# Nine of eleven swiglu blocks by seven products instead of eight, with six fill-in units in most turns and A12 ahead of F3

## The chip, the cores and the metric

One core of one Trainium2 chip. The metric is the device time of one execution in microseconds; lower is better. Times are the median of three runs. The profile is of one execution, with a span from the first to the last instruction.

## The reference

Two layers on an input of 256 tokens by 2048, fp32. Each layer adds a token mixer (a gated linear attention in layer 0, a sparse attention in layer 1) and then a swiglu, both on the RMS-normed input. Weights are read once from HBM. The change touches only the swiglu, with D_FF = 5632:

```
def swiglu(h, w1, w3, w2):
    return (jax.nn.silu(h @ w1) * (h @ w3)) @ w2

for i in range(DEPTH):                      # DEPTH = 2
    ...
    x = x + swiglu(rmsnorm(x, norm_ffn[i]), ffn_w1[i], ffn_w3[i], ffn_w2[i])
```

## The kernel before

All large products run in three fp32r matmuls: each operand is split into a high part and the rest, and hi*hi, hi*lo and lo*hi are added in PSUM. For weights this is `split_w`: a 1 MB tile (128 x 4 x 512) is cast on ACT to `wh` (line 137), then VectorE subtracts to get `wl` (line 138). `wh` and `wl` have three buffers each. Tiles that are used once come through the tag `raw`, which has four buffers (`RAW = 4`); the SP queue loads them. A unit of work that has 24 matmuls of 128x512 is called a step below.

The swiglu works on 11 blocks of 512 columns of w1 and w3. The tokens are two tiles of 128 and the inner dimension is cut in two halves, so that the pair (h @ w1 block, h @ w3 block) is a product of 2x2 block matrices:

- The plain way (`plain_steps`, matmuls at line 475, PSUM tile `half`) takes 8 block products, in 8 units of 24 matmuls each. Each unit splits one raw tile and uses it for both token tiles.
- The other way (`pair`, matmuls at line 398, PSUM tile `acc`) is a Strassen-Winograd form with 7 block products of 24 matmuls each, called A11, F5, F3, A12, F6, N7 and N22 after the combined activations that they use. Each product splits two weight tiles (chunk c = 0, 1), each for 12 matmuls. The combined weights are built on the way: `va` and `vb` are loaded to homes of their own (tags v0, v1, v2 and g3). During A11 VectorE adds `vb` to `va` (`plus`, line 411). During F5 and F6 POOL issues loads that add to `va` in flight (`plus_dma`, line 419). During F3 VectorE forms `-vb - vc` in `vb` (`minus`, line 415), `vc` being F3's own raw tiles; N7 reads the result. A12 has the raw tiles `vd`.

A sum on VectorE is not issued at once. `product` appends it to `sums_due`, and the next `split_w` issues it right behind its own subtraction:

```
        v = nc.vector.tensor_sub(wl, raw, wh.bitcast(F32))
        if sums_due:
            with behind((v.ins,)):
                sums_due.popleft()()
```

So the sum for F3's chunk 0 stands behind the split of F3's chunk 1, and that for chunk 1 behind the split of whatever comes next.

The down projection of finished blocks (`pieces`, matmuls at lines 531 to 533, PSUM tile `down`) is cut in units too, of one weight tile and 24 matmuls: four units a block. A piece of two blocks copies `x` into PSUM (line 521), runs two units, and copies back (line 538), four times; a piece of one block does so for every unit.

`ffn` runs the blocks with seven products one after the other, as turns. `pair` is a generator that yields after each product (slots 0 to 6) and once more (slot 7). After a slot, `ffn` calls `unit()` as many times as the slot stands in the turn's tuple, and each call takes the next unit from the list `todo`. Before, nearly every turn has a unit at each of the eight slots, two of them in a row at the end (slots 6 and 7). -1 in a tuple is a unit ahead of the turn. The gated results of a block are transposed in the following turn (`late`, `side`, `tick`, line 220) and kept in one of three tiles by `hi_lo(b % 3)`, until the down projection has read them. The last block's down projection is done after the turns.

The tile framework sets the order of the instructions in each engine's queue at build time from the program's order and from what is ready by its own estimate, and adds all semaphores. A tile is taken when its buffer is free.

Of the kernel before, what the change touches and what calls it, by code (L numbers as in the profile page):

```python
# [55 lines left out]
def trunk(  # L56
# [60 lines left out]
    def tick():  # L117

        while side:
            try:  # L120
                return next(side[0])
            except StopIteration:
                side.popleft()
# [9 lines left out]
    def split_w(raw, pool=wp):  # L133

        wh = pool.tile([P, 4, NB], F32R, tag="wh", bufs=3 if pool is wp else 1, name="wh")
        wl = pool.tile([P, 4, NB], F32R, tag="wl", bufs=3 if pool is wp else 1, name="wl")
        nc.scalar.copy(wh, raw)  # L137
# [4 lines that stand above are left out]
        return wh, wl  # L142
# [70 lines left out]
    def split_t(src, hi, lo):  # L213

        for kk in range(2):
            tr = tr_p.tile([P, 2, SEQ], F32, tag="tr", name="tr")
            for t in range(NT):
                for k in range(2):
                    c = (2 * kk + k) * P
                    nc.tensor.transpose(tr[:, k, t * P:(t + 1) * P], src[t][:, c:c + P], ident)  # L220
            sl = slice(2 * kk, 2 * kk + 2)
            nc.scalar.copy(hi[:, sl, :], tr)  # L222
            nc.vector.tensor_sub(lo[:, sl, :], tr, hi[:, sl, :].bitcast(F32))
            yield
# [139 lines left out]
    def hi_lo(i):  # L364
        g = res.tile([P, 2, 4, SEQ], F32R, tag=f"g{i}", name=f"g{i}")
        return g[:, 0], g[:, 1]
# [6 lines left out]
    def pair(nrm, wa, wb, c0, turn, done):  # L373

        def src(w, j, c):
            r = j * 1024 + c * 512
            return w[r:r + 512, c0:c0 + NB].rearrange("(k p) n -> p k n", p=P)

        def load(w, j, homes):
            o = []
            for c, (pool, tag, bufs) in enumerate(homes):
                raw = pool.tile([P, 4, NB], F32, tag=tag, bufs=bufs, name=tag)
                nc.sync.dma_start(raw, src(w, j, c))
                o.append(raw)
            return o

        def product(acc, raws, form, start, stop, then=None):
            for c in range(2):  # L390
                wh, wl = split_w(raws[c])
                if then is not None:
                    then(c)
                hi, lo = nrm.forms[form]
                for j in range(4):
                    k = 4 * c + j
                    for i, (l_, r_) in enumerate(((hi, wh), (hi, wl), (lo, wh))):
                        nc.tensor.matmul(acc, l_[:, k, :], r_[:, j, :], start=start and k == i == 0,  # L398
                                         stop=stop and k == 7 and i == 2, skip_group_check=not start)
                    if j % 2:  # L400
                        tick()

        def bank():
            return acc_p.tile([P, NB], F32, tag="acc", name="acc")

        def sums(tag):
            return nrm.pool.tile([P, NB], F32, tag=tag, bufs=1, name=tag)

        def plus(dst, other):

            return lambda c: sums_due.append(lambda: nc.vector.tensor_add(dst[c], dst[c], other[c]))  # L411

        def minus(dst, other):

            return lambda c: sums_due.append(lambda: nc.vector.scalar_tensor_tensor(
                dst[c], dst[c], -1.0, other[c], op0=ALU.mult, op1=ALU.subtract))

        def plus_dma(dst, w, j):
            return lambda c: nc.gpsimd.dma_start(dst[c], src(w, j, c), accum_op=ALU.add)

        fz = nrm.pool
        stream = [(wp, "raw", RAW)] * 2
        homes = [((fz, "v0", 1), (fz, "v1", 1)), ((fz, "v2", 1), (res, "g3", 1))]
        va = load(wa, 0, homes[turn])
        vb = load(wb, 0, homes[1 - turn])
        b1 = bank()
        product(b1, va, "A11", True, True, plus(va, vb))
        b3 = bank()
        nc.scalar.mul(b3, b1, -1.0)
        yield  # L430
        b2 = bank()
        product(b2, va, "F5", True, True, plus_dma(va, wb, 1))
        y = cm.tile([P, NB], F32, tag="u", name="u")
        nc.scalar.copy(y, b2)
        yield
        vc = load(wb, 1, stream)
        product(b2, vc, "F3", False, True, minus(vb, vc))
        yield
        vd = load(wa, 1, stream)
        product(b1, vd, "A12", False, True)  # L440
        done("11", b1)
        yield
        product(b3, va, "F6", False, True, plus_dma(va, wa, 1))
        w = sums("w")
        nc.scalar.copy(w, b3)
        nc.vector.tensor_add(w, w, b2)
        done("12", w)
        yield
        product(b3, vb, "N7", False, True)
        nc.vector.tensor_add(y, y, b3)  # L450
        yield
        product(b3, va, "N22", False, True)
        done("21", b3)
        done("22", y)
        yield
        yield
# [84 lines left out]
    def ffn(layer, nrm):  # L541

        w1, w3, w2 = ffn_w1[layer], ffn_w3[layer], ffn_w2[layer]
        sc = {}
        ready = set()
        late = []

        def block(b, us):
            def turned():
                yield from split_t(us, hi, lo)  # L550
                ready.add(b * NB)

            hi, lo = hi_lo(b % 3)
            late.append(turned())
            made[b] = hi, lo, b * NB

        def gate(us):
            def done(q, v):
                t = int(q[0]) - 1
                if q == "21":  # L560
                    nc.scalar.activation(v, v, AF.Silu, scale=sc["n"][:, 1:2])
                    us[t] = v
                elif q == "22":
                    nc.vector.scalar_tensor_tensor(v, v, sc["r"][:, 1:2], us[t], op0=ALU.mult, op1=ALU.mult)
                    us[t] = v
                elif q[1] == "1":
                    us[t] = cm.tile([P, NB], F32, tag="u", name="u")
                    nc.scalar.activation(us[t], v, AF.Silu, scale=sc["n" if t else "r"][:, t:t + 1])
                else:
                    nc.vector.scalar_tensor_tensor(us[t], us[t], sc["r"][:, t:t + 1], v, op0=ALU.mult, op1=ALU.mult)  # L570
            return done

        todo = deque()
        made = {}

        def unit():

            while True:
                kind, item, gen = todo[0]
                try:  # L580
                    got = next(gen)
                except StopIteration:
                    todo.popleft()
                    continue
                if got is not None:
                    made[item] = got[0]
                    late.append(got[1])
                return

        def filler(item):  # L590

            if isinstance(item, int):
                return "plain", item, plain_steps((w1, w3), item, nrm.forms, sc, ready)
            return "piece", item, pieces(w2, [made[b] for b in item], ready)

        full = (0, 1, 2, 3, 4, 5, 6, 7)
        turns = ((0, (-1, -1, 0, 1, 2, 4, 5, 6), (1,)), (2, full, ((1, 0),)), (3, full, (4,)), (5, full, ((2, 3),)),
                 (6, full, ((4, 5),)), (7, full, (8,)), (9, full, ((6, 7),)), (10, full, ((8, 9),)))
        for turn, (b, at, items) in enumerate(turns):
            todo.extend(filler(i) for i in items)  # L600
            us = [None] * NT
            for _ in range(at.count(-1)):
                unit()
            for slot, _ in enumerate(pair(nrm, w1, w3, b * NB, 1 - turn % 2, gate(us))):
                side.extend(late)
                late.clear()
                for _ in range(at.count(slot)):
                    unit()
                if turn == 0 and slot == 0:
                    flush()  # L610
                    sc["r"] = nrm.rstd()
                    sc["n"] = scaled(sc["r"], -1.0, "rq")
            block(b, us)
        for _, _, gen in todo:
            assert next(gen, None) is None
        side.extend(late)
        return w2, [made[10]]
# [557 lines left out]
```

## Time and profile before

| | |
|---|---|
| median of 3 runs | 2227.94 us (2227.71 to 2228.21) |
| the profiled execution's own time | 2227.94 us |
| its span | 2226.2 us |
| TensorE matmul busy | 2207.4 us |
| VectorE busy | 1545.1 us |
| ACT busy | 1289.2 us |
| data moved | 493.35 MB, mean 222 GB/s |

In the profile's rows PE is TensorE's matmuls, DVE is VectorE, ACT is ScalarE, and SPq and POOLq are the queues that issue loads. L398 is line 398 of the kernel. A timeline row has the start and the length in us, the engine, the line, the operation and its tiles, and in brackets the idle time before it and what ended it. A chain row has the start, the length and what was at work, with the number of instructions. Windows give the busy time of each engine in a stretch, the granted clock, the mean busy share of the 16 DMA engines, and GB/s. A row of waits has the total in us, the number of times and the longest. A matmul's own length in the trace is longer than its share of time, since matmuls overlap; the chain shows the share. A few matmul records can be missing.

### The profile page before, as it was taken

To read this page: it belongs to the slowest core of one execution; us is meant where nothing else is said; L and a number is where in the kernel's file an instruction comes from. 1 tells how busy PE (TensorE), PEld (TensorE's weight loads), DVE (VectorE), ACT (ScalarE), POOL (GpSimd) and SP (SyncE) were. 2 spreads that over 40 slices of the span, in tenths; PEclk is the share of its full clock that TensorE was granted. 3 is DMA by queue.
4 is the path that set the end of the run, shared out by engine and by line. 5 is a ranking of instruction groups with operands and counts; after the bars stand their busy time and mean duration, and the time that the engine had idled before them with its cause. 6 is when DMAs were issued, how large, how long until landed. Compare 5 with 4: busy or idle time off the path is not lost.

```text
span 2226.2 us, 25148 instructions
## 1 busy us (share of the span) xinstructions
PE 2207.4 (99%) x10199; PEld 1828.2 (82%) x10199; DVE 1545.1 (69%) x1180; ACT 1289.2 (58%) x1248; POOL 111.3 (5%) x157
## 2 busy tenths in 40 slices
PE   9999999999999999999999999999999999999998
PEld 7888888888888888888888888888888888888886
DVE  6546546887777777877655755557877777787776
ACT  5545445666656665666544445456666666666664
POOL 0000000000000000000100000000000000000000
PEclk9999999999999999999999999999999999999999
DMA  8555465889879879777554554466997897897893
GB/s 293 172 170 178 135 229 179 263 224 314 222 228 307 221 229 315 211 228 231 194 183 142 178 173 159 164 204 196 298 243 238 276 247 228 281 261 214 281 245 114
DMA packets 254773, 493.35 MB, mean 222 GB/s; under 512 B 8201, under 2 KB 20833, under 8 KB 254529
## 3 DMA queue, kind: packets, MB, share of 16 engines
q1 hardware_dynamic: 219856, 423.33, 54.4%
q0 software_dynamic: 33792, 67.11, 17.3%
q8 instruction: 80, 1.31, 0.2%
q10 hardware_dynamic: 1008, 1.31, 0.2%
q14 instruction: 37, 0.30, 0.0%
HBM read 489.59 MB, written 2.12 MB: 221 GB/s over the span
## 4 chain that ended last, share of the span: by engine, by line
PE 95%; DVE 2%; ACT 1%; issue 1%; DMA 0%; SPq 0%; POOL 0%; POOLq 0%; ACTq 0%
PE acc L398 26%; PE half L475 11%; PE acc L206 11%; PE acc L208 11%; PE acc L207 11%; PE down L533 7%; PE down L532 6%; PE down L531 6%; PE tr L220 1%; DVE wl L138 1%; ACT wh L137 1%; PE trq L906 0%; PE po L765 0%; DVE v L411 0%; PE s L750 0%
## 5 line engine op out<-in xcount | busy, mean ns | idle before, releaser
L138 DVE TENSOR_TENSOR wl<-raw,wh 128x2048 fp32r<-128x2048 f32 x193 | 441.4, 2291 | 229.8 <-ACT wh L137 228.9
L197 DVE TENSOR_TENSOR wl<-raw,wh 128x2048 fp32r<-128x2048 f32 (+3 forms) x147 | 317.7, 2164 | 275.7 <-ACT wh L196 275.6
L137 ACT CAST wh<-raw 128x2048 fp32r<-128x2048 f32 x193 | 369.4, 1914 | 203.1 <-PE half L475 71.7
L196 ACT CAST wh<-raw 128x2048 fp32r<-128x2048 f32 (+3 forms) x147 | 265.1, 1807 | 221.1 <-PE acc L208 191.1
L206 PE MATMUL acc<-wh,hh 128*128 128x512 f32 (+3 forms) x832 | 325.4, 391 | 0.0
L208 PE MATMUL acc<-wh,hl 128*128 128x512 f32 (+3 forms) x832 | 317.3, 381 | 0.0
L207 PE MATMUL acc<-wl,hh 128*128 128x512 f32 (+3 forms) x832 | 316.4, 380 | 0.6 <-DVE wl L197 0.6
L138 DVE TENSOR_TENSOR wl<-v,wh 128x2048 fp32r<-128x2048 f32 x120 | 274.0, 2289 | 45.1 <-ACT wh L137 44.8
L137 ACT CAST wh<-v 128x2048 fp32r<-128x2048 f32 x120 | 229.7, 1914 | 71.6 <-PE acc L398 35.3
L532 PE MATMUL down<-wl,g 128*128 128x512 f32 x640 | 249.6, 390 | 1.1 <-DVE wl L138 1.1
L531 PE MATMUL down<-wh,g 128*128 128x512 f32 x640 | 249.6, 391 | 0.9 <-ACT g L507 0.9
L533 PE MATMUL down<-wh,g 128*128 128x512 f32 x640 | 248.5, 390 | 0.6 <-DVE g L508 0.6
L207 PEld LDWEIGHTS acc<-wl,hh 128*128 128x128 f32 x832 | 156.7, 188 | 29.6 <-issue 1.7
L208 PEld LDWEIGHTS acc<-wh,hl 128*128 128x128 f32 x832 | 156.3, 188 | 29.3
L206 PEld LDWEIGHTS acc<-wh,hh 128*128 128x128 f32 x832 | 156.5, 188 | 28.6 <-issue 1.9
L398 PE MATMUL acc<-wh,fhF 128*128 128x512 f32 x384 | 150.8, 393 | 0.0
L398 PE MATMUL acc<-wh,flF 128*128 128x512 f32 x384 | 149.9, 390 | 0.0
L398 PE MATMUL acc<-wl,fhF 128*128 128x512 f32 x384 | 149.6, 390 | 0.0
L532 PEld LDWEIGHTS down<-wl,g 128*128 128x128 f32 x640 | 120.2, 188 | 27.6 <-DVE wl L138 2.8
L531 PEld LDWEIGHTS down<-wh,g 128*128 128x128 f32 x640 | 120.2, 188 | 26.1 <-ACT g L507 1.5
L533 PEld LDWEIGHTS down<-wh,g 128*128 128x128 f32 x640 | 119.9, 188 | 26.2 <-DVE g L508 1.4
L206 PE MATMUL acc<-wh,g 128*128 128x512 f32 x312 | 123.3, 395 | 0.7 <-ACT g L222 0.7
(283 smaller groups left out, 3675.9 us busy)
## 6 DMA issues: line engine op xcount, KB each, us to landing
raw<-in_ffn_w SPq DMA_DIRECT2D x200, 1024.0 KB, 6.2
v<-in_ffn_w SPq DMA_DIRECT2D x48, 1024.0 KB, 8.4
v<-in_ffn_w POOLq DMA_DIRECT2D x48, 1024.0 KB, 9.9
raw<-in_dsa_w_in SPq DMA_DIRECT2D x48, 1024.0 KB, 4.9
raw<-in_gla_w_in SPq DMA_DIRECT2D x40, 1024.0 KB, 5.0
raw<-in_gla_w_out SPq DMA_DIRECT2D x16, 1024.0 KB, 5.0
g<-in_ffn_w SPq DMA_DIRECT2D x16, 1024.0 KB, 8.0
g<-in_ffn_w POOLq DMA_DIRECT2D x16, 1024.0 KB, 13.8
```

The source lines that it names most:

```text
L137: nc.scalar.copy(wh, raw)
L138: v = nc.vector.tensor_sub(wl, raw, wh.bitcast(F32))
L196: a = nc.scalar.copy(wh[:, sl, :n], raw[:, sl, :n])
L197: v = nc.vector.tensor_sub(wl[:, sl, :n], raw[:, sl, :n], wh[:, sl, :n].bitcast(F32))
L206: nc.tensor.matmul(acc[t][:, :n], hi[:, k, ts_], wh[:, k, :n], start=start, stop=False)
L207: nc.tensor.matmul(acc[t][:, :n], hi[:, k, ts_], wl[:, k, :n], start=False, stop=False)
L208: nc.tensor.matmul(acc[t][:, :n], lo[:, k, ts_], wh[:, k, :n], start=False, stop=last)
L398: nc.tensor.matmul(acc, l_[:, k, :], r_[:, j, :], start=start and k == i == 0, stop=stop and k == 7 and i == 2, skip_group_check=not start)
L475: nc.tensor.matmul(acc[bank], l_[:, k, :], r_[:, j, :], start=start and k == i == 0, stop=stop and k == 7 and i == 2, skip_group_check=not ...
L531: nc.tensor.matmul(acc[t], hi[:, k, ts_], wh[:, k, :], start=False, stop=False, skip_group_check=True)
L532: nc.tensor.matmul(acc[t], hi[:, k, ts_], wl[:, k, :], start=False, stop=False, skip_group_check=True)
L533: nc.tensor.matmul(acc[t], lo[:, k, ts_], wh[:, k, :], start=False, stop=last, skip_group_check=True)
```

## The change

One more block of each layer goes from the plain way to seven products: turns for blocks 0, 2, 3, 4, 6, 7, 8, 9 and 10 instead of 0, 2, 3, 5, 6, 7, 9 and 10, and plain blocks 1 and 5 instead of 1, 4 and 8. The units are 56 instead of 64 a layer, dealt out over nine turns: 7 in the first (two of them ahead), 5 in the second, 6 in each of the following, and 8 in the last. The tuples leave slots 2 and 7 empty in all turns but the last; those of blocks 0 and 2 leave slot 6 empty too. Within `pair`, A12 moves ahead of F3, so that slot 2 now lies between A12 and F3, and slot 3 between F3 and F6. Blocks 0 and 9 are down-projected in pieces of one block.

```
         y = cm.tile([P, NB], F32, tag="u", name="u")
         nc.scalar.copy(y, b2)
         yield
-        vc = load(wb, 1, stream)
-        product(b2, vc, "F3", False, True, minus(vb, vc))
-        yield
         vd = load(wa, 1, stream)
         product(b1, vd, "A12", False, True)
         done("11", b1)
+        yield
+        vc = load(wb, 1, stream)
+        product(b2, vc, "F3", False, True, minus(vb, vc))
         yield
         product(b3, va, "F6", False, True, plus_dma(va, wa, 1))
...
-        full = (0, 1, 2, 3, 4, 5, 6, 7)
-        turns = ((0, (-1, -1, 0, 1, 2, 4, 5, 6), (1,)), (2, full, ((1, 0),)), (3, full, (4,)), (5, full, ((2, 3),)),
-                 (6, full, ((4, 5),)), (7, full, (8,)), (9, full, ((6, 7),)), (10, full, ((8, 9),)))
+        five, six = (0, 1, 3, 4, 5), (0, 1, 3, 4, 5, 6)
+        turns = ((0, (-1, -1, 0, 1, 3, 4, 5), (1,)), (2, five, ((0,),)), (3, six, ((1, 2),)), (4, six, (5,)),
+                 (6, six, ((3, 4),)), (7, six, ()), (8, six, ((5, 6),)), (9, six, ((7, 8),)),
+                 (10, (0, 1, 2, 3, 4, 5, 6, 7), ((9,),)))
```

A turn's tuple has a block, its slots and the items that join `todo`: a number is a plain block, a tuple of numbers a piece of the down projection.

## The prediction

> **What bounds the kernel now.** I read the page's totals and the chain that ended last, then stretches, then one turn of the swiglu by chain and by engine.
>
> ```profile
> span 2226.2 us, 25148 instructions
> PE 2207.4 (99%) x10199; PEld 1828.2 (82%) x10199; DVE 1545.1 (69%) x1180; ACT 1289.2 (58%) x1248; POOL 111.3 (5%) x157
> ...
> q1 hardware_dynamic: 219856, 423.33, 54.4%
> q0 software_dynamic: 33792, 67.11, 17.3%
> ...
> PE 95%; DVE 2%; ACT 1%; issue 1%; DMA 0%; SPq 0%; POOL 0%; POOLq 0%; ACTq 0%
> ```
>
> TensorE is the bound: 99% busy, 95% of the chain. The two queues give the price of a load: 54.4% of the span for 423.33 MB is 3.0 us of all DMA engines for one 1 MB tile (1.049 million bytes); 17.3% for 67.11 MB is 6.0 us for a tile added in flight by POOL, twice as much.
>
> ```profile
> core 0: us, PE busy (x) PEld busy (x) DVE busy (x) ACT busy (x) POOL busy (x), PEclk, DMA share, GB/s
> 561.80:644.30 82.50, 82.50 (x369) 68.34 (x368) 63.23 (x35) 49.15 (x36) 5.16 (x4) 1.00 0.86 255
> 571.60:588.10 16.50, 16.50 (x74) 13.64 (x73) 13.50 (x8) 9.07 (x7) 2.54 (x2) 1.00 0.96 196
> 395.00:1061.00 666.00, 664.45 (x2969) 548.21 (x2968) 514.34 (x283) 422.66 (x341) 43.51 (x38) 1.00 0.84 251
> ```
>
> One swiglu takes 666 us. In a turn of it (the second row) nothing makes TensorE wait, but VectorE is busy 77% and the DMA engines 86%, and right after the first pair of POOL's adding loads the DMA engines are full (0.96).
>
> ```profile
> 573.76 5.44 PE acc L398 x24
> 579.21 5.44 PE half L475 x24
> 584.64 5.44 PE acc L398 x24
> 590.09 5.44 PE half L475 x24
> ...
> PE down L532 <- DVE wl L138: 1.1, 4, 0.3
> ```
>
> The chain gives the grid on which I place everything: a product and a unit both have 24 matmuls and take 5.44 us. The last row is the largest wait of TensorE for a split weight tile: 1.1 us in the whole program.
>
> **The change part by part.** *One block fewer by the plain way.* Per layer a block goes from 8 units (192 matmuls) to 7 products (168). Transposes stay. That is 24 matmuls or one step of 5.44 us per layer: 2 x 5.44 = 10.9 us off the path, if TensorE stays as full. *Work beside it.* The block gains 6 splits and 4 sums on VectorE, 10 instructions of about 2.29 us, and 4 adding loads (24 us of DMA). A turn with six units has 13 steps and 0.9 us of transposes (82.5 - 15 x 5.44), 71.6 us. VectorE keeps 63.2 - 2 x 2.29 = 58.6 us of it (82%), the DMA engines 0.86 x 82.5 - 2 x 3.0 = 65 us (91%). On the mean both still fit, so all depends on the order inside a turn. *Pieces of one block* (0 and 9) add 32 PSUM copies on ACT in all, about 0.6 us each, off the path while ACT is busy 423 of 666 us. Block 6 needs the tile of block 3 until the turn after it; it is read first a turn later, so that wait costs nothing.
>
> *The unit taken from behind A12.* Now A12 and F3 stand side by side, and F3's sums come right before the next unit. I use the quoted turn's grid: U1 from 579.21 to 584.64; in the changed kernel A12 follows to 590.09, F3 to 595.52, and then unit U3. These rows give the delays:
>
> ```profile
> 579.73 1.92 ACT L137 CAST wh<-raw 128x2048 fp32r<-128x2048 f32 x1
> 584.68 1.92 ACT L137 CAST wh<-raw 128x2048 fp32r<-128x2048 f32 x1 [2.13 <-PE half L475]
> 588.16 1.91 ACT L137 CAST wh<-raw 128x2048 fp32r<-128x2048 f32 x1 [1.56 <-DMA raw<-in_ffn_w]
> 591.44 1.92 ACT L137 CAST wh<-raw 128x2048 fp32r<-128x2048 f32 x1 [1.36 <-DMA raw<-in_ffn_w]
> ...
> 578.47 2.29 DVE L138 TENSOR_TENSOR wl<-raw,wh 128x2048 fp32r<-128x2048 f32 x1 [0.39 <-ACT wh L137]
> 581.67 2.29 DVE L138 TENSOR_TENSOR wl<-raw,wh 128x2048 fp32r<-128x2048 f32 x1 [0.91 <-ACT wh L137]
> 583.88 2.28 DVE L415 SCALAR_TENSOR_TENSOR v<-v,raw 128x2048 f32<-128x2048 f32 x1
> 586.63 2.29 DVE L138 TENSOR_TENSOR wl<-raw,wh 128x2048 fp32r<-128x2048 f32 x1 [0.47 <-ACT wh L137]
> 588.84 2.28 DVE L415 SCALAR_TENSOR_TENSOR v<-v,raw 128x2048 f32<-128x2048 f32 x1
> ```
>
> A cast waits until TensorE is done with the tile three before (584.68 against the step's end at 584.64); the split's second half ends 4.24 us after the cast starts (584.68 to 586.63 + 2.29); a sum and a split in a row take 2.2 us each (581.67, 583.88). So in the changed kernel F3's second cast may start when A12's first half is done, 587.36 + 0.04, and its split ends at 591.64. The program puts F3's first sum right behind that on VectorE: 593.84. Queued behind it is U3's split, which ends at 596.05. TensorE wants U3 at 595.52: it waits 0.53 us. In the kernel before a unit stood ahead of F3, whose step gave VectorE the time, and the same sum cost nothing. Without a sum four half products in a row are harmless: in turn 0 of the kernel before A12 and F6 stand side by side,
>
> ```profile
> 438.93 10.88 PE acc L398 x48
> ...
> 446.92 2.29 DVE L138 TENSOR_TENSOR wl<-raw,wh 128x2048 fp32r<-128x2048 f32 x1 [1.00 <-ACT wh L137]
> ```
>
> and the next unit's split ends at 449.21, 0.6 us ahead of the step's end at 449.81. A sum of 2.2 us there goes past that.
>
> *The loads that F3 needs.* There are four raw buffers, so a load goes out when the fourth raw tile before it is split. Before, the load that waited for U1's split was A12's first; now the order of raw tiles is U0, U1, two for A12, two for F3, and it is F3's second, which is wanted 8.2 us earlier (595.52 became 592.81 on the grid, the cast 587.40).
>
> ```profile
> 578.11 0.37 SPq L385 DMA_DIRECT2D raw<-in_ffn_w  x1
> ...
> DMA to landing us min/median/max: 10.0/10.0/10.0
> ...
> 586.24 0.37 SPq L385 DMA_DIRECT2D raw<-in_ffn_w  x1
> ...
> L385 SPq DMA_DIRECT2D raw<-in_ffn_w x1: 368/368/368, 2127.2 to 2127.2; - x1
> DMA to landing us min/median/max: 11.1/11.1/11.1
> ...
> L385 SPq DMA_DIRECT2D raw<-in_ffn_w x1: 368/368/368, 994.1 to 994.1; - x1
> DMA to landing us min/median/max: 12.4/12.4/12.4
> ```
>
> The load of 578.11 was let out by U1's split (ending 578.11), shared the engines with POOL's pair, and landed after 10.0 us; the same load of the last turn took 11.1, of another turn 12.4. The next one, at 586.24 with the pair done, was used at 591.44: 5.2 us. With a latency t the cast starts at 578.16 + t, U3's split is ready 4.24 + 2 x 2.2 = 8.65 us later, and TensorE has waited t - 8.7 us in all (part before F3's second half, the rest before U3). That is 1.3 us for 10.0, 2.4 for 11.1, 3.7 for 12.4. The range of this term is 0 (all filled) to 3.7; I take 2.4, since the row of the last turn lies in the middle of such loads. Eight turns of nine lack that unit (all but the last), in two layers: 16 x 2.4 = 38.4 us.
>
> [...]
>
> *Turns 0 and 2 end without a unit,* so N22 meets the next A11. These rows give what comes in addition there:
>
> ```profile
> 633.64 0.66 ACT L561 ACTIVATE acc<-acc,rq 128x512 f32<-128x512 f32 x1 [0.80 <-PE acc L398]
> 635.08 0.74 DVE L564 SCALAR_TENSOR_TENSOR u<-u,rstd,acc 128x512 f32<-128x512 f32 x1
> ```
>
> From N22's start: A11's second cast at 2.76, split done 7.0, the gate's multiply 0.65 more, A11's first sum until 9.85, the unit's split until 12.05, and TensorE wants it at 10.88: 1.2 us, in 2 places of 2 layers, 4.7 us. Before, a unit stood there in every turn. Bounds 0 and 1.9 each (a silu before the cast).
>
> *Sum.* -10.9 + 38.4 + 4.7 = +32.2 us. The profiled execution took 2227.94 us (span 2226.2 and 1.7 around it), and that is the median too: 2260 us.
>
> **The rivals.** *The waits are filled, and it gets faster.* The build orders TensorE's queue by its own estimate of what is ready, and mixes two steps in places:
>
> ```profile
> 662.14 0.69 PE acc L398 x3
> 662.82 0.24 PE down L531
> ...
> 663.76 0.93 PE acc L398 x4
> ```
>
> F3, F6 and a unit write different banks, so matmuls of a later step could stand in the waits of F3 and U3, for no time at all. Against it: the split that the later step needs stands in VectorE's queue behind the very sum and the late split that TensorE waits for, and the sums of before follow their split at once (583.88, 588.84). It decides when what is left of the wait is under (10.9 - 4.7) / 16 = 0.4 us a turn. Time: 2227.94 - 10.9 + 4.7 = 2221.7, or 2217.1 with the ends of turns filled too.
>
> [...]
>
> *The DMA engines become the bound.* At 91% a turn has 6.6 us to spare. U3's load and the next now go out beside the first pair as well, so the adding loads may land late for F6 and N22: by up to one load of 3.0 us per turn. At half of that, in 18 turns, 27 us more: about 2287. For it speaks the full stretch of the second window row, against it the mean over a turn.
>
> **How the numbers follow.** Forecast 0.57 (its own range 2242 to 2272, from 10.0 us and about 11.8 us of latency as means over the turns), filled waits 0.23, load in time 0.12, DMA bound 0.08. About 0.2% (4.5 us) can be told from no change. Faster is the first rival with the lower edge of the second, 0.25; same is nearly all of the second, 0.10; slower 0.65. The range 2219 to 2271 leaves out most of the DMA case, part of the first rival and the forecast's upper edge.
>
> **What would show it.** TensorE should have 48 matmuls less and the waits "half" and "down" for the second half of a split (line 138), some 1.7 us each, about 16 times, and "acc" line 398 for the same, about 0.6 us. The sums at line 415 should stand between F3's second split and the unit's. The second load of F3 should leave at U1's split and take 10 to 12 us, with ACT waiting for it. Steps should stay at 5.44 us. I am wrong if these waits are missing (the order on VectorE then is another), or if the load lands within 9 us.

## The result, and the profile after

The changed kernel takes 2256.16 us (median of 4 runs, 2254.45 to 2256.27) where the kernel before takes 2227.93 us on the same chip: a ratio of 1.0125, with a 95% interval of 1.0107 to 1.0142. It is 28.2 us slower; 32.2 had been predicted. The profiled execution took 2256.13 us.

These are the lines of the page of the changed kernel that answer to those of before, first the totals, then the queues, then the chain that ended last:

```profile
span 2254.4 us, 25134 instructions
...
PE 2210.8 (98%) x10151; PEld 1821.1 (81%) x10151; DVE 1589.2 (70%) x1200; ACT 1324.5 (59%) x1294; POOL 121.6 (5%) x165
...
q1 hardware_dynamic: 219856, 423.33, 53.3%
q0 software_dynamic: 38016, 75.50, 18.9%
...
PE 74%; DMA 11%; DVE 7%; issue 4%; ACT 3%; SPq 0%; POOL 0%; ACTq 0%; POOLq 0%; DVEq 0%
```

TensorE has 48 matmuls fewer and still ends later: the chain, which ran 95% through TensorE, now runs 11% through DMA transfers and 7% through VectorE. The waits of TensorE in the changed kernel (total in us, times, longest) say for what it waits:

```profile
PE acc L398 <- DVE wl L138: 13.3, 14, 1.8
PE down L532 <- DVE wl L138: 6.4, 7, 0.9
PE half L475 <- DVE wl L138: 5.6, 7, 0.9
...
PE acc L398 <- ACT wh L137: 2.9, 3, 1.5
```

A product (L398) waits for the second half of a split, and 14 times so does a unit (L532 and L475). Together the four rows are 28.2 us, where the largest such row of before was 1.1. That this is also the net loss is chance: the net has the saving of 10.9 us in it, and smaller losses that are no waits. All of the added time lies in the two swiglus. The windows from the first to the last matmul of each, first of the kernel before and then of the changed one:

```profile
394.30:1060.90 666.60, 665.05 (x2971) 548.69 (x2970) 515.04 (x284) 423.16 (x341) 43.51 (x38) 1.00 0.84 250
1527.60:2194.10 666.50, 665.21 (x2971) 548.82 (x2971) 514.86 (x284) 423.13 (x341) 42.67 (x34) 1.00 0.84 251
```

```profile
394.30:1076.50 682.20, 668.12 (x2954) 546.54 (x2952) 537.72 (x295) 441.32 (x365) 48.67 (x42) 0.99 0.85 251
1541.90:2223.40 681.50, 666.96 (x2954) 545.20 (x2952) 537.63 (x295) 441.30 (x366) 47.84 (x38) 1.00 0.85 251
```

That is 15.6 + 15.0 = 30.6 us more in the swiglus, and 2.4 less around them, because six of the last block's eight transposes, which stood behind the last unit before, now stand ahead of it. The 30.6 can be split by taking the trace's start-to-start time of each matmul against 0.2267 us (5.44 / 24): -10.9 for the 48 matmuls, +38.1 for time lost between and within matmuls (49.3 us after, 11.2 before), +3.4 for transposes.

How one turn loses it is seen in the fourth turn, that of block 4. Rows of the changed kernel's timeline, of SyncE's queue, ScalarE, VectorE and TensorE in turn:

```profile
640.62 0.37 SPq L385 DMA_DIRECT2D raw<-in_ffn_w  x1
...
651.76 1.91 ACT L137 CAST wh<-raw 128x2048 fp32r<-128x2048 f32 x1 [1.72 <-DMA raw<-in_ffn_w]
...
653.71 2.29 DVE L138 TENSOR_TENSOR wl<-raw,wh 128x2048 fp32r<-128x2048 f32 x1 [1.33 <-ACT wh L137]
655.92 2.28 DVE L415 SCALAR_TENSOR_TENSOR v<-v,raw 128x2048 f32<-128x2048 f32 x1
658.12 2.28 DVE L138 TENSOR_TENSOR wl<-raw,wh 128x2048 fp32r<-128x2048 f32 x1
...
659.13 0.39 PE L398 MATMUL acc<-wh,fhF 128*128 128x512 f32 x1
660.46 0.50 PE L475 MATMUL half<-wl,fhA 128*128 128x512 f32 x1 [0.94 <-DVE wl L138]
```

F3's second load leaves at 640.62, when the first unit's split has ended, and its cast waits for it until 651.76. Then come the split, F3's first sum (L415) and only then the next unit's split (658.12 to 660.40), for which TensorE stands still until 660.46. The trace's answer for that one load:

```profile
L385 SPq DMA_DIRECT2D raw<-in_ffn_w x1: 368/368/368, 640.6 to 640.6; - x1
...
DMA to landing us min/median/max: 11.0/11.0/11.0
```

The changed kernel holds its own control. The last turn of each layer keeps the unit between A12 and F3. In the second layer's last turn, the same load is just as slow:

```profile
L385 SPq DMA_DIRECT2D raw<-in_ffn_w x1: 368/368/368, 2158.7 to 2158.7; - x1
...
DMA to landing us min/median/max: 11.4/11.4/11.4
```

From the chain of the same stretch:

```profile
2162.57 5.44 PE acc L398 x24
2168.01 0.23 PE down L531
...
2173.45 5.44 PE acc L398 x24
2178.89 0.23 PE down L531
```

A12, the unit, F3 and the next unit follow each other without a hole (2168.01 = 2162.57 + 5.44, 2173.45 = 2168.01 + 24 x 0.2267, 2178.89 = 2173.45 + 5.44). The latency is the same and costs nothing; only the missing unit makes it count.

### The profile page after: what moved, and what is told of

It reads as the page before. It is cut to its first block, busy times and chain, and to the rows that moved or that the text cites. A ratio compares the mean times of both kernels' runs of the same rounds, so it can differ in the third digit from the quotient of the medians.

```text
span 2254.4 us, 25134 instructions
## 1 busy us (share of the span) xinstructions
PE 2210.8 (98%) x10151; PEld 1821.1 (81%) x10151; DVE 1589.2 (70%) x1200; ACT 1324.5 (59%) x1294; POOL 121.6 (5%) x165
## 2 busy tenths in 40 slices
DMA packets 258995, 501.73 MB, mean 223 GB/s; under 512 B 8328, under 2 KB 20960, under 8 KB 258752
## 4 chain that ended last, share of the span: by engine, by line
PE 74%; DMA 11%; DVE 7%; issue 4%; ACT 3%; SPq 0%; POOL 0%; ACTq 0%; POOLq 0%; DVEq 0%
PE acc L398 16%; PE acc L206 11%; PE acc L208 11%; PE acc L207 11%; DMA raw<-in_ffn_w 9%; PE half L475 6%; DVE wl L138 5%; PE down L532 5%; PE down L533 5%; PE down L531 5%; ACT wh L137 3%; DMA g<-in_ffn_w 2%; PE tr L220 1%; PE trq L907 0%; PE po L766 0%
## 5 line engine op out<-in xcount | busy, mean ns | idle before, releaser
L138 DVE TENSOR_TENSOR wl<-raw,wh 128x2048 fp32r<-128x2048 f32 x185 | 423.5, 2291 | 239.6 <-ACT wh L137 239.5
L137 ACT CAST wh<-raw 128x2048 fp32r<-128x2048 f32 x185 | 353.8, 1913 | 207.9 <-PE down L533 68.3
L138 DVE TENSOR_TENSOR wl<-v,wh 128x2048 fp32r<-128x2048 f32 x132 | 300.8, 2288 | 31.6 <-ACT wh L137 30.7
L137 ACT CAST wh<-v 128x2048 fp32r<-128x2048 f32 x132 | 252.6, 1913 | 75.5 <-PE acc L398 29.5
L532 PE MATMUL down<-wl,g 128*128 128x512 f32 x640 | 250.5, 391 | 6.5 <-DVE wl L138 6.4
L398 PE MATMUL acc<-wl,fhF 128*128 128x512 f32 x432 | 172.5, 399 | 13.5 <-DVE wl L138 13.3
L398 PE MATMUL acc<-wh,fhF 128*128 128x512 f32 x432 | 171.1, 396 | 3.0 <-ACT wh L137 2.9
L398 PE MATMUL acc<-wh,flF 128*128 128x512 f32 x432 | 170.2, 394 | 0.0
L532 PEld LDWEIGHTS down<-wl,g 128*128 128x128 f32 x640 | 120.1, 188 | 35.0 <-DVE wl L138 10.6
L419 POOL DMA_DIRECT2D v<-in_ffn_w x52 | 67.3, 1294 | 1168.0 <-DVE wl L138 1017.5
## 6 DMA issues: line engine op xcount, KB each, us to landing
v<-in_ffn_w SPq DMA_DIRECT2D x54, 1024.0 KB, 10.1
```

The costliest lines, as they stand in the source:

```text
L532: nc.tensor.matmul(acc[t], hi[:, k, ts_], wl[:, k, :], start=False, stop=False, skip_group_check=True)
```

## The experiments

Theory A is that of the prediction: a turn loses time because F3's second load is late (it runs beside POOL's adding pair) and because F3's first sum stands ahead of the next unit's split; the missing unit between A12 and F3 exposes both. Theory B knows the late load alone. Theory C says that the DMA engines are full on the mean, so that a wait taken away in one place comes back in another. All ratios are to the kernel before, timed beside each run.

**The sums one split later (sums_later).**

```
-        product(b2, vc, "F3", False, True, minus(vb, vc))
+        held = []
+        product(b2, vc, "F3", False, True, held.append)
+        for c in held:
+            minus(vb, vc)(c)
```

> The changed kernel, with F3's two sums each one split later on VectorE: the first behind the next unit's split instead of ahead of it. Theory A (two causes: F3's second load leaves too late, and the sum stands ahead of the unit's split): the unit's waits of about 0.9 us in 14 turns go and F3's own waits stay, so 13 to 16 us come back: 2240 to 2244 us. Rival B (one cause, the late load; the unit's split would be late anyway): within 3 us of 2256. Rival C (the DMA engines are full on the mean over a turn, and waits come up wherever they can): within 3 us of 2256, with the same total of waits elsewhere.

Measured: 2248.97 us, 1.0094 (1.0079 to 1.0109), 7.2 us under the changed kernel, about half of what A expected. TensorE's waits for splits in this kernel:

```profile
PE acc L398 <- DVE wl L138: 16.9, 27, 1.8
...
PE acc L398 <- ACT wh L137: 2.5, 3, 1.1
```

The units (L475, L532) have left the list, so the sum did cause their waits. F3's own waits stay, and there are 13 waits more on products: the sum now stands ahead of one of F6's splits, which it makes late. Moving the sum moved its price in part: 12.0 us of waits of units went, 3.6 us of waits of products came.

**Without the first pair (no_first_pair).** F5's two adding loads are left out, so the tiles that F6 and N22 read lack that term.

```
-        product(b2, va, "F5", True, True, plus_dma(va, wb, 1))
+        product(b2, va, "F5", True, True)
```

> The changed kernel without the two loads that POOL adds to va during F5 (so va lacks one of its terms and the products with F6 and N22 have other values). Theory A: F3's second load has the engines to itself and lands in 5 to 6 us, in time; about 0.5 us a turn stays for the sum: 2227.9 - 10.9 + 8.5 = 2225.5, 2222 to 2230 us. Rival D (the load is late because of its buffer alone, whatever runs beside it): within 3 us of 2256. Rival C: something between, since 16 of some 100 us of DMA work a layer go.

Measured: 2223.24 us, 0.998 (0.9971 to 0.9989). Its waits:

```profile
PE down L532 <- DVE wl L138: 3.3, 10, 0.4
PE acc L398 <- DVE wl L138: 1.6, 5, 0.4
```

In every turn F3's second load now lands 4.9 to 6.1 us after its issue, and F3 waits only in the second turn of each layer, 0.5 us. What stays is ten waits of units, 0.48 to 0.58 us each from one matmul's start to the next beyond 0.2267: the sum alone, for which the prediction worked out 0.53 us. So it is the pair beside it that makes the load late, and not its buffer alone.

**Without the first pair, and the sums later (no_first_pair_sums_later).** Both edits above together.

> The changed kernel without POOL's first pair of adding loads (left out: the term that they add to the tiles of F6 and N22), and with F3's sums one split later. Theory A: neither cause is left: 2217 us, 6 us under the kernel without the pair alone (2223.2). Theory B: 2223, no change against that kernel.

Measured: 2218.0 us, 0.9954 (0.9939 to 0.997). Of the waits for splits only one row is left:

```profile
PE acc L398 <- DVE wl L138: 1.5, 5, 0.4
```

With the load in time and the sum out of the way the whole saving of 10.9 us is nearly there (2227.93 - 10.9 = 2217.0). Here, with F6's tiles early, the moved sum cost nothing. Theory B, which gave the sum no part, expected 2223.2 and is out.

**Holding the pair back, in three attempts (pair_later, pair_held, pair_held_sums_later).** The same loads, but later. In pair_later they are written after A12's first split, in pair_held behind a small copy on POOL that reads F3's second raw tile (its edit is shown), and the third is pair_held with the sums later.

```
-        product(b2, va, "F5", True, True, plus_dma(va, wb, 1))
+        product(b2, va, "F5", True, True)
...
         vc = load(wb, 1, stream)
+        hold = nrm.pool.tile([P, 1], F32, tag="hold", bufs=1, name="hold")
+        nc.gpsimd.tensor_copy(hold, vc[1][:, 3, 511:512])
+        for i in range(2):
+            plus_dma(va, wb, 1)(i)
```

> The changed kernel with F5's two adding loads issued after A12's first split instead of after F5's splits, so that F3's second load goes ahead of them. All data and work as before. Theory A: that load lands within 7 us of U1's split, about 0.5 us a turn stays for the sum: 2223 to 2230 us; if F6's casts must now wait for the adding loads, up to 2240. Rival C (full DMA engines): within 3 us of 2256, since no byte is saved.

> The changed kernel, but POOL's first pair of adding loads stands behind a small POOL copy that reads F3's second raw tile, so the pair really starts only once that tile has landed. The same bytes are moved. Theory A (two causes: F3's second load is late because it runs beside the pair; and F3's first sum stands ahead of the next unit's split): the load takes about 5 us, F3's waits go, about 0.5 us per turn in 16 turns stays (8 us): 2222 to 2230 us, and the second adding load, which then lands some 18 to 20 us after the hold, is just in time for F6 (waits there of up to 1 us would put it at 2230 to 2240). Theory B (late load only): 2217. Theory C (the DMA engines are full on the mean): the wait moves to F6 and the time stays at 2250 or more.

> The pair held as in the kernel pair_held, and F3's two sums each one split later on VectorE as in sums_later. Theory A: the load's wait is gone and the sum's wait moves to F6, which has a unit's step before it: 2217 to 2224 us, at or under the kernel with the pair held alone. Theory B: the same as with the pair held alone within 2 us. Theory C: 2245 or more.

Measured: 2255.33 us (1.0123, 1.0108 to 1.0139), 2256.09 us (1.0125, 1.011 to 1.014) and 2247.42 us (1.0087, 1.0072 to 1.0103), the times of the changed kernel and of sums_later again. These are no verdict on A. The first adding load of the swiglu, on POOL's timeline of the changed kernel, of pair_later and of pair_held, one fence each:

```profile
415.62 1.51 POOL L419 DMA_DIRECT2D v<-in_ffn_w  x1 [15.06 <-DVE wl L138]
```

```profile
415.47 1.51 POOL L419 DMA_DIRECT2D v<-in_ffn_w  x1 [15.07 <-DVE wl L138]
```

```profile
415.50 1.51 POOL L419 DMA_DIRECT2D v<-in_ffn_w  x1 [15.06 <-DVE wl L138]
```

It leaves at the same moment, within 0.15 us, in all three. Nothing in the data tied the pair to what was written ahead of it, and the build put it where it could start.

**The pair really tied (pair_tied, pair_tied_sums_later).** Ahead of each adding load stands a POOL product that reads the tile it adds to, so the load must follow it, and F3's second raw tile.

```
-        product(b2, va, "F5", True, True, plus_dma(va, wb, 1))
+        product(b2, va, "F5", True, True)
...
+        for i in range(2):
+            hold = nrm.pool.tile([P, 1], F32, tag=f"hold{i}", bufs=1, name="hold")
+            nc.gpsimd.tensor_tensor(hold, va[i][:, 3, 511:512], vc[1][:, 3, 511:512], op=ALU.mult)
+            plus_dma(va, wb, 1)(i)
```

> The changed kernel, with POOL's first pair of adding loads really held: ahead of each stands a POOL product of one column of the tile that it adds to and one of F3's second raw tile, so the load has to wait for F3's second load to land (in pair_held and pair_later the build issued the pair at the old time, so those two tell nothing). The same bytes are moved. Theory A (late load plus sum ahead of the unit's split): F3's second load takes 5 to 7 us in place of 10 to 14, F3's waits go, about 1 us per turn stays for the sum: -10.9 + 16 x 0.5 to 1.0, 2225 to 2233 us; but the second adding load lands about 17 us after the hold, within 1 or 2 us of F6's need, which can give back up to 1.5 us x 16, 2233 to 2250. Theory B (late load only): 2217 plus the same give-back. Theory C (the DMA engines are full on the mean): the wait only moves, 2250 or more.

> The same hold, with F3's two sums one split later on VectorE. Theory A: both causes gone, 2217 to 2222 us plus what a late second adding load costs F6 (up to 1.5 us x 16); some 8 us under pair_tied. Theory B: the same as pair_tied within 2 us. Theory C: 2245 or more.

Measured: 2264.41 us (1.0161, 1.0145 to 1.0177) and 2271.05 us (1.0192, 1.0176 to 1.0208): slower than the changed kernel, a miss for A's numbers, and the order of the two is reversed. Both times lie where theory C had them (2250 and 2245 us or more); what speaks against C is old_order_slot3, below. The load's part of A is borne out all the same. F3's second load in pair_tied, in the turn that was shown above:

```profile
L385 SPq DMA_DIRECT2D raw<-in_ffn_w x1: 368/368/368, 637.1 to 637.1; - x1
...
DMA to landing us min/median/max: 4.9/4.9/4.9
```

In all 18 turns it takes 4.9 to 6.2 us, with the same bytes in the program as the changed kernel. But the pair is now late for F6. ScalarE in that turn, and below it TensorE's waits in pair_tied:

```profile
655.13 1.90 ACT L137 CAST wh<-v 128x2048 fp32r<-128x2048 f32 x1 [3.05 <-DMA v<-in_ffn_w]
661.83 1.91 ACT L137 CAST wh<-v 128x2048 fp32r<-128x2048 f32 x1 [4.80 <-DMA v<-in_ffn_w]
```

```profile
PE acc L398 <- ACT wh L137: 25.9, 17, 2.1
PE acc L398 <- DVE wl L138: 10.5, 19, 1.0
```

The adding loads were issued at 643.90 and 644.69 and landed 11.1 and 17.0 us later. I had reckoned with F6's second tile 1 to 2 us late; both are, and F6's first matmul stands ahead of the unit in TensorE's queue, so the unit waits with it. In pair_tied_sums_later a sum stands ahead of F6's second split as well, the place that is now the tight one (29.2 us of waits of products for VectorE's half of a split). But all its waits for casts and splits are some 36 us, against some 38 in pair_tied, so they do not reverse the order. What differs is the clock: its mean over a run was 0.991 to 0.993 in the four runs of pair_tied_sums_later and 0.995 to 0.999 in those of pair_tied (0.993 and 0.998 in the profiled ones). The 0.5% between those two is 11 us of 2268, and the medians lie 6.6 us apart (the last section has more on the clock). So this hold is no cure: within one turn the pair would have to be early for F6 and late for F3.

**Another empty slot (old_order_slot3, new_order_slot3, old_order), and the order alone (order_alone).** In the first, nine blocks by seven products keep the old order A11 F5 F3 A12 F6 N7 N22, and slot 3, between A12 and F6, is left empty in place of slot 2. The second leaves slot 3 empty in the new order (between F3 and F6), the third slot 2 in the old order (between F3 and A12). order_alone is the kernel before with the new order of products. The lines are the edit of the second against the changed kernel; the first has the same turns.

```
-        five, six = (0, 1, 3, 4, 5), (0, 1, 3, 4, 5, 6)
-        turns = ((0, (-1, -1, 0, 1, 3, 4, 5), (1,)), (2, five, ((0,),)), (3, six, ((1, 2),)), (4, six, (5,)),
+        five, six = (0, 1, 2, 4, 5), (0, 1, 2, 4, 5, 6)
+        turns = ((0, (-1, -1, 0, 1, 2, 4, 5), (1,)), (2, five, ((0,),)), (3, six, ((1, 2),)), (4, six, (5,)),
```

> Nine blocks by seven products, with the order of before (A11 F5 F3 A12 F6 N7 N22) and the missing unit taken from slot 3 instead of slot 2, so that A12 and F6 stand side by side and F3 keeps a unit on either side. Theory A: no sum of VectorE and no late load meets the close pair; the 10.9 us come out, less what the ends of turns 0 and 2 cost: 2216 to 2221 us. Rival C: the ninth block itself is too much for DMA and VectorE: 2245 us or more. Rival E (the ninth block is to blame for a part, the order for a part): 2225 to 2240.

> The changed kernel with the unit missing behind F3 instead of behind A12, so that a unit stands between A12 and F3, and F3 and F6 stand side by side. F3's second load is then let out one step earlier against its use. Theory A: the late load goes; F3's first sum now stands ahead of F6's split and costs 0.5 to 1 us in 16 turns, 8 to 16 us: 2225 to 2233 us. Theory B (late load only): 2217. Theory that any missing unit in the middle costs the same: 2250 or more.

> The changed kernel's turns (nine blocks, unit missing behind the third product) with the old order of products, so F3 and A12 stand side by side, and the late load is A12's second. Theory A: the load let out by U1's split is again the second of the next product's after the pair, one product later than F3's was, but the sums of F3 stand ahead of A12's split: the load leaves 5 us more, the sum costs 0.5 to 1 us per turn, and A12's two splits follow at once: 2235 to 2262 us. Theory B (late load of the fourth raw tile only): 2240 to 2256. A theory that the new order is itself the fault: 2217 to 2225.

> The kernel before (its turns with a unit behind every product, seven blocks by seven products), with the new order of products alone. A unit stands between A12 and F3 and between F3 and F6, so neither the load nor the sum is short of time: all theories that put the cost on the missing unit expect 2226 to 2231 us, the same as before. If the order itself costs (F3's load, the pair's deadline for F6), it is 2235 or more.

| nine blocks | old order | new order |
|---|---|---|
| slot 2 empty | 2246.46 us, 1.0083 (1.0065 to 1.0101): F3 beside A12 | 2256.16 us, 1.0125 (1.0107 to 1.0142): A12 beside F3 |
| slot 3 empty | 2216.9 us, 0.995 (0.9933 to 0.9967): A12 beside F6 | 2235.73 us, 1.0036 (1.0023 to 1.0049): F3 beside F6 |

order_alone takes 2230.5 us, 1.0011 (1.0002 to 1.0021): the new order by itself costs some 2.5 us. The price is set by which two products lose the unit between them. A12 beside F6 is the one pair with no sum of VectorE ahead of a split that is wanted at once and with no late load. It gives the whole saving, and a kernel faster than both: but for one wait of 0.2 us, its only waits for VectorE's half of a split are

```profile
PE acc L398 <- DVE wl L138: 1.7, 5, 0.5
```

It moves the same 501.73 MB as the changed kernel in 39 us less, so theory C is out: the DMA engines are not the bound. With F3 beside F6 the load has a step more time, and what is left is mostly the sum ahead of F6's split; TensorE's waits of new_order_slot3:

```profile
PE acc L398 <- DVE wl L138: 12.6, 20, 1.2
```

The 2235.73 us lie 3 above A's range. The time of old_order lies in the ranges of both A and B and decides nothing between them, but it rules out that the new order is itself the fault (2217 to 2225 us). Its trace showed something that I had only half foreseen. The chain that ended last, in one turn of old_order:

```profile
644.45 1.71 DVE v L415
646.16 0.02 SPq L467
...
646.23 5.15 DMA raw<-in_ffn_w
...
651.48 1.92 ACT wh L137
```

A sum reads the raw tile too, so the buffer comes free at the end of the sum, one VectorE instruction after the split; the unit's load leaves only then, and the unit waits for its cast. TensorE's waits of old_order:

```profile
PE down L531 <- ACT wh L137: 13.9, 10, 2.7
PE half L475 <- ACT wh L137: 4.8, 6, 1.4
```

## Why the prediction came out as it did

*The sign and the mechanism were right.* F3's second load leaves at U1's split, takes 10.1 to 11.9 us in the ordinary turns, and the cast, the split, the sum and the unit's split follow in the order that was worked out. Theory A's two causes are shown separately: the sum (0.48 to 0.58 us in ten of sixteen turns with the load in time, and 5.2 us between the two kernels without the pair), and the load (the pair left out: 33 us less; tied: nearly no wait in F3, and the loss is F6's).

*The wait of 2.4 us x 16 was right in the sum but not in its parts.* The time lost between and within matmuls is 38.1 us, ends of turns included. The waits of units are 14 of 0.9 us, not 16 of 1.7, and those of products 14 of 1.0, not 0.6. For t = 11.0 us the formula t - 8.7 gives 2.3; the turn shown has 1.1 before the unit and about 0.5 in small holes. The build put two matmuls of the unit ahead of F3's last one (0.45 us of work, the rival "waits are filled" in small), and U1's split was 1.4 us ahead of its step (640.59 to 642.01) instead of 1.1. Over the twelve ordinary turns the trace's holes of over 0.2 us come to 1.6 us on the mean. The second and third turn of each layer make up for it with 3.7 to 5.4 us each: there F3's second load takes 12.4 to 14.2 us, and the half clock of the last section is in it, some 5 us in all, which the prediction did not have. So it is in part luck that 38.1 lies next to 38.4: the ordinary turns lost less than was forecast, four turns lost more. The prediction had one row as long (12.4) and took it for the upper end of every turn, not for the usual thing in two turns of nine.

*The ends of turns (4.7 us) were too large.* The term failed at the step that let TensorE want the unit as soon as A11 was done. The rows of VectorE at the end of block 2's turn:

```profile
549.37 2.28 DVE L411 TENSOR_TENSOR v<-v,v 128x2048 f32<-128x2048 f32 x1
551.57 2.28 DVE L138 TENSOR_TENSOR wl<-raw,wh 128x2048 fp32r<-128x2048 f32 x1
```

The sum does delay the unit's split, which ends at 553.85, but the eight transposes of the block before stand at the unit's start on TensorE (552.54 to 553.58) and fill most of it; two starts of matmuls in a row there lose about 0.5 us. In the kernel with the same turn ends and no other loss, 2216.9 us, nothing of 4.7 us can be seen.

*Of the rivals,* "load in time" is the one in which F3's second load holds nothing up and only the sum counts: 2230.2 by the prediction's own terms (2227.94 - 10.9 + 16 x 0.53 + 4.7). Made true by leaving the pair out, it gives 2223.2, and the difference is the 4.7 us and some turns in which the sum costs nothing; with the pair in place the load took 10.1 us or more in every turn of the changed kernel. "DMA engines the bound" (2287) is ruled out by 2216.9 us with the same bytes. "Waits are filled" happened for 0.45 us a turn.

*The claims at no cost held.* Block 6's tile shows no wait, and ScalarE's extra copies (46 instructions more) show none: of the three waits of a product for ScalarE, 2.9 us in all, two (1.47 and 0.99) are the late cast of F3's second tile in the third turns.

## What to carry to other kernels

A unit of independent work between two steps does more than fill the bound engine: it gives the other engines' queues and the loads one step more of time (5.44 us here), and taking it away is priced by what then stands between the two neighbours. Count, for each candidate place, the vector instructions between the two steps and the load that gets let out there, and take the filler from the place with neither; here the choice of place and order was worth 39 us, against a saving of 11. A load that lands too late in a turn can look harmless in the profile of before (no wait of TensorE at a latency of 11 us), so latencies should be read along with the slack that covers them.

## What the runs showed of the hardware

*In the changed kernel the clock fell three times after waits of under 2 us.* After the second and third turns' waits matmuls ran 0.427 us apart instead of 0.227. Windows of the changed kernel (length, then busy time of PE, PEld, DVE, ACT and POOL, the granted clock, DMA share, GB/s):

```profile
508.00:511.00 3.00, 1.33 (x6) 1.10 (x7) 3.00 (x2) 3.00 (x3) 0.00 (x0) 0.99 0.36 139
511.00:514.00 3.00, 3.00 (x9) 2.35 (x8) 3.00 (x3) 1.24 (x2) 0.00 (x0) 0.50 0.20 21
514.00:517.00 3.00, 3.00 (x14) 2.49 (x13) 3.00 (x3) 1.66 (x1) 0.00 (x0) 0.95 1.04 403
...
582.50:585.50 3.00, 3.00 (x8) 2.33 (x9) 3.00 (x2) 2.24 (x2) 0.00 (x0) 0.52 0.01 2
```

A stretch with TensorE 44% busy was followed by about 3 us at half the clock, with eight matmuls of 0.2 us more: 1.6 us on top of a wait of 1.8. It happened three times (also near 1730), some 5 us of the 28.2, and the prediction, which held steps at 5.44 us, did not have it. It did not happen in the second layer's second turn, after the same wait of 1.8 us and a stretch of 3 us in which TensorE was 39% busy (1655 to 1658), nor after single waits of about 1 us. In the trace's record of the granted clock each of the three lasts 3.41 us, and their starts, at 510.92, 582.60 and 1729.47, lie 21 and 336 times 3.413 us apart. In the 3.41 us right ahead of them TensorE was 48% (1.63 us), 20% (0.67) and 22% (0.76) busy; from 1654.38 to 1657.79 it was 46% (1.58 us) busy, and the full clock followed. So the busy share of such a stretch does not by itself tell the cases apart, and what does is not shown by these runs.

*Beside the pair, F3's second load moved about as many bytes as the pair, a third of its own pace behind it.* F3's second load took 10.1 to 14.2 us beside the pair and 4.9 to 6.2 us without it. The DMA packets in the trace of the changed kernel show where the time goes. In the sixteen turns without the unit its first packet starts 3.7 to 4.5 us after the issue; in no_first_pair and pair_tied that is 1.0 us, and so it is for the loads of the changed kernel that find their queue idle and no pair under way. From then on, while the pair is under way, the queue of the load moves 130 to 141 KB/us and that of the pair 125 to 130 (in the turn shown above, from 645 to 650, 0.69 MB and 0.64). Once the pair is done, the queue of the load moves 382 to 406 KB/us (from 652 to 655, 1.22 MB). The bytes are about equal, the time of a packet is not: a 2 KB packet of the pair takes 176 ns and one of the load beside it 98 ns. Why the load's first packet starts some 3 us later beside the pair is open.
